# Six units' output rows evicted by ScalarE and added to x by GpSimd; V products one slot later, in a one-core encoder layer

## The chip, the cores and the metric

One Trainium2 chip, of which one core is used. The metric is the device time of one execution in microseconds, as the median of several runs; less is better. Beside the runs stands one profiled execution with its trace: each engine's instructions, their start, their length, and what ended the idle time before them. TensorE (PE in the profile, PEld its weight loads) multiplies, VectorE (DVE), ScalarE (ACT) and GpSimd (POOL) compute, SyncE (SP) issues nearly all transfers. Every engine works through its own instructions in order.

## The reference

One encoder layer over 1024 positions (a grid of 16 rows by 64 columns) of width 1024. x is RMS-normalised and projected to 3328 columns. Group A is attention of every position to every position (8 heads, 2 shared key/value heads, normalised and rotated q and k); group B lets a position see a window of 8 rows and 16 columns. Each group is multiplied by a SiLU gate, both are concatenated, projected once more, added to x and normalised:

```python
h = _rmsnorm(x, norm_gain[l])
proj = h @ w_in[l]
q_a, k_a, v_a, g_a, q_b, k_b, v_b, g_b = jnp.split(proj, split_at, axis=-1)
o_a = _gqa_blocked(q_a, k_a, v_a) * jax.nn.silu(g_a)
o_b = _neighbourhood_attn(q_b, k_b, v_b, na_rpb[l]) * jax.nn.silu(g_b)
x = x + jnp.concatenate([o_a, o_b], axis=-1) @ w_out[l]
return _rmsnorm(x, final_norm_gain)
```

(heads' reshapes, the norm and rotation of q_a and k_a left out). All is float32; the kernel splits every factor of a product into two float16 parts, high and low, and sums three products.

## The kernel before, in words

The 1024 positions are eight *units* of 128 rows (u); the unit's rows are chosen so that a unit of group B sees only itself and its neighbours, two units of keys at the borders, three elsewhere. Weights come in 17 groups of 256 columns: 0 to 12 of the first projection, 13 to 16 of the output projection. Every group is loaded (`load_w`), its sum of squares is formed in four quarters by ScalarE (`squares`, L372), and then it is split: high parts by ScalarE (L414), low parts by VectorE (L419). A unit's 24 matmuls with one group fill half a PSUM bank (`proj_tile`; two banks in turn in this stage, three in the tail).

The stage that the change touches is group B's (363 to 509 us): 32 *pairs* of heads, four for each unit in `ORDER` (0, 7, 1, 2, 3, 4, 5, 6). `run_units` walks through numbered *slots*. In slot i:

- `b_lo` (L863) forms the low half of pair i-1's weights on VectorE, and SP sends both halves through a transposing DMA (L865) into one of three `ptb` buffers;
- `b_qk` makes pair i's scores on TensorE (L833, L836), their biased row maxima on VectorE (L854), exponentials (L856) and high half (L858) on ScalarE;
- TensorE does about 4.2 *chunks* of fill, six matmuls each (L504): first the gate projections (groups 11 and 12), then the output projection, one *generator* of 8 chunks for two blocks of 128x256;
- `b_pv` multiplies pair i-3 with V on TensorE (L883 to L885). After four heads VectorE evicts the result (L892 to L895), GpSimd multiplies it with the gate (L897).

When a unit has both its halves, `os_start` squares, scales and splits its row of 1024 (L920, L925, L928, L933, L937) and SP transposes it (L946); these are the left factors of the output projection. An output generator (`out_gen`) ends with `then`, which files a job: `add` evicts the two blocks on VectorE, scaled row by row and added to x (L994). Then come squares of the finished half row on ScalarE (`fin_a`, L1019), the norm (`fin_b`, L1026 to L1030) and the store (L1031). x is loaded anew (`load_x2`, L984).

The order on an engine is that in which the program issues. `Flow.step` issues a slot: jobs of ScalarE up to 1.2 us of cost, then b_lo and b_qk, then the other jobs of ScalarE, jobs of VectorE, fill, and b_pv. A slot has a budget of 2.85 us for ScalarE's jobs and 2.45 for VectorE's (from `BASE_B`), of which up to half a budget is carried on; a job's `cost` is charged against it. Jobs with `late=0` always go in the slot where they are due, in the order of filing; others (squares of an output weight group: 1.0 each; its high parts 0.6, group 14's 0.3; its low parts 1.0) wait when the budget is short. The split of a unit's row counts 0.72 twice on ScalarE, `add` 0.5 a block on VectorE. Once a unit's job is filed it is due a slot later unless a delay is given.

Group B's stage ends with slot 34. Behind it the remaining output generators run back to back (the tail).

Of the kernel before, what the change touches and what calls it, by code (L numbers as in the profile page):

```python
# [8 lines left out]
F32 = mybir.dt.float32  # L9
F16 = mybir.dt.float16  # L10
BF16 = mybir.dt.bfloat16
AF = mybir.ActivationFunctionType
OP = mybir.AluOpType
# [3 lines left out]
P = 128  # L17
KC = 8
NU = 8
GC = 256  # L20
# [2 lines left out]
NX = 4  # L23
BASE_A, BASE_B = (1.72, 2.6, 2.8), (1.7, 1.6, 2.0)
HAND = 6
SKEW_A, SKEW_B = 5, 3
FILL_A = [(4, 5.0), (7, 4.2)]
FILL_A_END = 3.6
CHUNKS_A = 264
# [10 lines left out]
SLOTS = {"both": (16384, 2048, 4), "qc": (24576, 2048, 2), "stg1": (28672, 2048, 3), "stg": (18432, 2048, 3),  # L40
         "t": (0, 3072, 3), "ptb": (9216, 3072, 3), "th": (32896, 2048, 1), "y": (32896, 2048, 1),
         "p32": (AREA + 14464, 3072, 1)}
ORDER = (0, 7, 1, 2, 3, 4, 5, 6)
# [4 lines left out]
class Flow:  # L48
# [17 lines left out]
    def job(self, eng, cost, fn, *a, delay=1, late=1, key=None):  # L66

        self.jobs.append((late, self.slot + delay, self.number(), eng, cost, fn, a, key, self.tail))
# [83 lines left out]
def kernel(ctx: ExitStack, tc: tile.TileContext, x: bass.AP, w: bass.AP, wo: bass.AP,  # L152
# [3 lines left out]
    act, dve, pool, pe, sp = nc.scalar, nc.vector, nc.gpsimd, nc.tensor, nc.sync  # L156
# [3 lines left out]
    whl = ctx.enter_context(tc.tile_pool(name="whl", bufs=2))  # L160
# [7 lines left out]
    at, job = fl.at, fl.job  # L168
# [4 lines left out]
    def rows_of(t, u, width, off, n):  # L173

        return dap(t, 8 * u * width + off, [[64 * width, 16], [width, 8], [1, n]])
# [5 lines left out]
    def carve(store, off, shape, dt):  # L181

        n = 4 if dt == F32 else 2
        t = store[:, off // 4:off // 4 + int(np.prod(shape)) * n // 4]
        t = t if n == 4 else t.bitcast(dt)
        if len(shape) == 1:
            return t
        names = "abcdef"[:len(shape)]
        return t.rearrange(f"p ({' '.join(names)}) -> p {' '.join(names)}", **dict(zip(names, shape)))

    def area(off, shape, dt):
        return carve(ar, off + 16384, shape, dt)

    turn = {}

    def slot(kind, shape, dt):

        off, size, n = SLOTS[kind]
        k = turn[kind] = turn.get(kind, -1) + 1
        off += k % n * size  # L200
        return area(off, shape[1:], dt) if off < AREA else carve(rq, off - AREA, shape[1:], dt)
# [9 lines left out]
    def tn(name, n=1, tag="t"):  # L211
        return tiny.tile([P, n], F32, tag=tag, name=name)


    raw, wp, late, x2 = {}, {}, {}, {}
# [24 lines left out]
    for c in range(2):  # L240
        cs = slice(c * 512, (c + 1) * 512)
# [20 lines left out]
    def col(i, n=1):  # L262
        return sm[:, i:i + n]
# [65 lines left out]
    def proj_tile(name):  # L329
        if not banks:  # L330
            return ps_p.tile([P, 2, GC], F32, tag="pj", name=name)
        if not own:
            own.extend(ps_p.tile([P, 2, GC], F32, tag="pj", name=f"pjb{i}") for i in range(2))
        if "tail" in late and len(own) < 3:
            own.insert(0, banks[3].rearrange("p (a b) -> p a b", b=GC))
        own.append(own.pop(0))
        return own[-1]
# [117 lines left out]
    def need_w(g):  # L455
        if g not in scaled:
            fl.need(("sq", g), lambda: g in pend or g in scaled)
            fl.urgent()
            sums_now(True)
        fl.need(g, lambda: g in ready)  # L460
# [40 lines left out]
    def chunks(ops, n, then=None):  # L501
        for i in range(0, len(ops), n):
            for o in ops[i:i + n]:
                pe.matmul(*o[0], **o[1])  # L504
            if i + n >= len(ops):
                (then or sums_now)()
            elif 2 * i + 2 * n == len(ops) == 24 and n == 3:
                sums_now()
            yield
# [298 lines left out]
    def keys(u):  # L808

        a = max(u - 1, 0)  # L810
        return a, min(u + 1, NU - 1) - a + 1
# [49 lines left out]
    def b_lo(u, p):  # L861
        hl, p32 = hls.pop(("b", u, p))
        dve.scalar_tensor_tensor(hl[:, 1], p32, 2.0 ** 14, hl[:, 0], op0=OP.mult, op1=OP.subtract)  # L863
        pt = slot("ptb", [P, 4 * keys(u)[1], P], F16)
        sp.dma_start_transpose(pt, hl.rearrange("p a k -> p (a k)"))  # L865
        pts["b", u, p] = pt

    def b_pv(u, p):
        pt = pts.pop(("b", u, p))
        n = keys(u)[1]  # L870
        for e in range(2):
            b_pv_head(u, 2 * p + e, pt[:, e * n:e * n + n], pt[:, (2 + e) * n:(3 + e) * n])
# [108 lines left out]
    def load_x2(u):  # L981
        if u not in loaded:
            loaded.add(u)
            sp.dma_start(x2[u], rows_of(x, u, 1024, 0, 1024))  # L984

    def out_gen(jobs, done=()):

        pt = proj_tile(f"po{jobs[0][0]}_{jobs[0][1]}")
        rw = tn(f"rw{jobs[0][0]}_{jobs[0][1]}", 2, "rw")
        def add():  # L990
            for i, (u, g) in enumerate(jobs):
                cs = slice((g - 13) * GC, (g - 12) * GC)
                load_x2(u)
                dve.scalar_tensor_tensor(x2[u][:, cs], pt[:, i], rw[:, i:i + 1], x2[u][:, cs], op0=OP.mult, op1=OP.add)  # L994
        def then():
            job("dve", 0.5 * len(jobs), add, late=0)
            for u, h in done:
                job("act", 0.82, fin_a, u, h, delay=2, late=2)

        for i, (u, g) in enumerate(jobs):  # L1000
            need_w(g)
            fl.need(("os", u), lambda: u in mT)
            if i == 0 and jobs[-1] == (u, g + 1) and g + 1 in ready:
                dve.tensor_tensor(rw, col(RC + g, 2), rws[u][:, 3:4].to_broadcast([P, 2]), op=OP.mult)
            elif i == 0 or not both:
                dve.tensor_tensor(rw[:, i:i + 1], rws[u][:, 3:4], col(RC + g), op=OP.mult)
            both = i == 0 and jobs[-1] == (u, g + 1) and g + 1 in ready
            hi, lo = wp[g]
            seq = [(mT[u][a][:, k], b[:, k]) for k in range(KC) for a, b in ((0, hi), (0, lo), (1, hi))]
            yield from chunks([((pt[:, i], l, r), dict(start=n == 0, stop=n == 23))  # L1010
                               for n, (l, r) in enumerate(seq)], 6, then if i == len(jobs) - 1 else None)
# [52 lines left out]
    k, q = [kva_gen(up) for up in UP], group(1, [qa_gen(0, up) for up in UP])  # L1064
# [104 lines left out]
    ub = [(u, p) for u in ORDER for p in range(NH // 2)]  # L1169
# [27 lines left out]
    a, b = ORDER[2:4]  # L1197
# [7 lines left out]
    def hooks2(i):  # L1205
        hooks(i)
        for u, k in zip(ORDER, SPLIT_AT):
            if i - SKEW_B == k:
                at(0, "post", os_start, u)

    for u in ORDER[4:7]:
# [3 lines left out]
    def parts_b(i, back):  # L1215
        def first():
            if 1 <= i <= 32:
                b_lo(*ub[i - 1])
            if i < 32:
                b_qk(*ub[i])  # L1220
        return first, None, (lambda: b_pv(*ub[i - back])) if i >= back else None

    with run_units(32, SKEW_B, parts_b, rates(FILL_B, FILL_B_END), hooks2):
        pass
# [93 lines left out]
```

## Time and profile before

| | |
|---|---|
| median of 3 runs | 556.71 us (555.53 to 557.19) |
| the profiled execution | 558.52 us |
| its span, first to last instruction | 556.7 us |
| TensorE busy | 511.8 us, granted clock 0.981 on average |
| VectorE, ScalarE, GpSimd busy | 448.4, 373.5, 162.4 us |
| scores of pairs 0, 17 and 31 on TensorE | from 363.8, 430.2 and 494.0 us |
| last product with V | 508.5 us |
| last matmul | ends at 548.5 us |

In an instruction's row stand its start, its length, engine, line, operation, output<-inputs, shapes and the number merged into one row; in brackets the idle time of the engine before it and what ended it. Names are those of the storage: `ar`, `rq` and `rest` are arrays that hold many things by turns (transposed weights of attention, for one, are in `ar`), `pjb` and `sb` are PSUM banks, `whl` and `rest` hold split weights.

### The profile page before, as it was taken

To read this page: it belongs to the slowest core of one execution; us is meant where nothing else is said; L and a number is where in the kernel's file an instruction comes from. 1 tells how busy PE (TensorE), PEld (TensorE's weight loads), DVE (VectorE), ACT (ScalarE), POOL (GpSimd) and SP (SyncE) were. 2 spreads that over 40 slices of the span, in tenths; PEclk is the share of its full clock that TensorE was granted. 3 is DMA by queue.
4 is the path that set the end of the run, shared out by engine and by line. 5 is a ranking of instruction groups with operands and counts; after the bars stand their busy time and mean duration, and the time that the engine had idled before them with its cause. 6 is when DMAs were issued, how large, how long until landed. Compare 5 with 4: busy or idle time off the path is not lost.

```text
span 556.7 us, 12839 instructions
## 1 busy us (share of the span) xinstructions
PE 511.8 (92%) x5071; PEld 398.3 (72%) x5071; DVE 448.4 (81%) x911; ACT 373.5 (67%) x647; POOL 162.4 (29%) x185
## 2 busy tenths in 40 slices
PE   2667989989999999999999999999999989899994
PEld 0456878777887555568888888988777867688883
DVE  4599689789987988879879898777988988988532
ACT  5546465967887878787696796558688769662211
POOL 2385888571010000101001022633622211214000
PEclk9979999998999999999999999999999989999998
DMA  8998738779999999999997989644797999988612
GB/s 245 213 193 228 132 58 209 116 143 179 209 195 206 199 218 188 202 194 174 201 212 165 185 178 211 98 124 113 118 202 119 161 238 233 179 142 181 180 40 75
DMA packets 244509, 95.40 MB, mean 171 GB/s; under 512 B 235489, under 2 KB 236001, under 8 KB 242530
## 3 DMA queue, kind: packets, MB, share of 16 engines
q1 hardware_dynamic: 242434, 81.23, 78.3%
q0 software_dynamic: 1728, 12.58, 7.3%
q10 hardware_dynamic: 288, 0.79, 0.5%
q8 instruction: 39, 0.64, 0.5%
q14 instruction: 20, 0.16, 0.1%
HBM read 29.56 MB, written 4.19 MB: 61 GB/s over the span
## 4 chain that ended last, share of the span: by engine, by line
PE 52%; DVE 9%; ACT 6%; DMA 4%; issue 4%; POOL 1%; SPq 0%; DVEq 0%; POOLq 0%; ACTq 0%
PE pj L504 18%; PE pjb L504 8%; PE kb L504 7%; PE pv L775 5%; PE s L741 4%; PE s L743 4%; ACT rq L856 3%; PE pv L776 2%; DVE ar L854 2%; ACT ar L858 2%; PE sb L504 2%; DMA pt<-ar 2%; DMA x2b<-in_x_dram 1%; DVE ar L863 1%; DMA ar<-ar 1%
## 5 line engine op out<-in xcount | busy, mean ns | idle before, releaser
L504 PEld LDWEIGHTS <-hT 128*128 128x128 f16 x2112 | 204.3, 99 | 57.7 <-issue 16.0
L504 PE MATMUL pj<-whl,hT 128*128 128x256 f16 x1680 | 202.2, 279 | 20.2 <-DMA hT<-ar 7.5
L752 ACT ACTIVATE ar<-s,nm,sm 128x1024 f32<-128x1024 f32 x64 | 77.0, 1203 | 48.3 <-DVE nm L748 47.1
L748 DVE CUSTOM_DVE_ANT_0 ar<-s,sm 128x1024 bf16<-128x1024 f32 x64 | 81.9, 1280 | 30.1 <-PE s L743 28.4
L504 PEld LDWEIGHTS <-ar 128*128 128x128 f16 x768 | 74.5, 99 | 15.6 <-issue 4.5
L758 DVE TENSOR_TENSOR ar<-ar 128x1024 f16<-128x1024 f32 x64 | 79.1, 1237 | 1.4 <-ACT ar L753 1.3
L753 ACT ACTIVATE ar<-ar 128x1024 f16<-128x1024 f32 x64 | 67.6, 1057 | 2.3 <-DVE ar L758 0.4
L504 PE MATMUL pjb<-whl,ar 128*128 128x256 f16 x480 | 57.9, 277 | 3.1 <-DVE x2b L994 2.1
L856 ACT ACTIVATE rq<-ar,nm 128x384 f32<-128x384 f32 (+1 forms) x64 | 34.2, 580 | 32.8 <-DVE nm L854 32.1
L504 PE MATMUL pjb<-whl,hT 128*128 128x256 f16 x432 | 50.4, 273 | 0.1
L504 PE MATMUL kb<-hT,whl 128*128 128x512 f16 x192 | 44.5, 379 | 0.0
L784 POOL TENSOR_TENSOR ar<-ar,sum 128x256 f32<-128x256 f32 x16 | 11.4, 710 | 111.6 <-DVE ar L783 96.3
L419 DVE SCALAR_TENSOR_TENSOR whl<-raw,sm,whl 128x512 f16<-128x512 f32 x52 | 40.1, 798 | 2.8 <-ACT whl L414 2.8
L741 PE MATMUL s<-kTa,rq 128*128 128x512 f16 x128 | 38.5, 383 | 0.9 <-ACT ar L752 0.9
L775 PE MATMUL pv<-va,ar 128*128 128x128 f16 x384 | 39.3, 220 | 0.0
L775 PEld LDWEIGHTS <-ar 128*128 128x128 f16 x384 | 34.1, 98 | 5.5 <-issue 0.3
L776 PE MATMUL pv<-va,ar 128*128 128x64 f16 x384 | 38.0, 193 | 0.0
L897 POOL TENSOR_TENSOR ar<-ar,qkg 128x256 f32<-128x256 f32 x16 | 18.6, 1159 | 64.5 <-DVE qkg L895 63.2
L776 PEld LDWEIGHTS <-ar 128*128 128x128 f16 x384 | 33.4, 98 | 5.5 <-issue 0.3
L863 DVE SCALAR_TENSOR_TENSOR ar<-rq,ar 128x768 f16<-128x768 f32 (+1 forms) x32 | 30.5, 954 | 7.4 <-ACT ar L858 7.2
L414 ACT ACTIVATE whl<-raw,sm 128x512 f16<-128x512 f32 x52 | 34.0, 709 | 1.4 <-POOL sm L391 1.4
L391 POOL TENSOR_TENSOR sm<-wss,mh 128x1 f32<-128x1 f32 x17 | 10.5, 619 | 74.0 <-DVE wss L390 74.0
(165 smaller groups left out, 892.0 us busy)
## 6 DMA issues: line engine op xcount, KB each, us to landing
raw<-in_w_dram POOLq DMA_DIRECT2D x11, 1024.0 KB, 7.6
ar<-in_x_dram SPq DMA_DIRECT2D x7, 512.0 KB, 6.3
raw<-in_wo_dram SPq DMA_DIRECT2D x3, 1024.0 KB, 6.6
khh<-ar SPq DMA_DIRECT2D x16, 128.0 KB, 2.5
x2b<-in_x_dram SPq DMA_DIRECT2D x4, 512.0 KB, 6.9
x<-in_x_dram SPq DMA_DIRECT2D x4, 512.0 KB, 5.4
out_dram<-x2b SPq DMA_DIRECT2D x8, 256.0 KB, 3.7
out_dram<-x SPq DMA_DIRECT2D x7, 256.0 KB, 2.9
```

Source lines behind the costliest of these rows:

```text
L414: act.activation(wp[g][0][:, q], raw[g][:, q], AF.Copy, scale=col(S_ + g))
L419: dve.scalar_tensor_tensor(wp[g][1][:, q], raw[g][:, q], col(S_ + g), wp[g][0][:, q], op0=OP.mult, op1=OP.subtract)
L504: pe.matmul(*o[0], **o[1])
L741: pe.matmul(s[:, c * 512:(c + 1) * 512], q, kTa[:, 4 * c:4 * c + 4, hh], start=True, stop=False)
L748: dve.tensor_tensor_reduce(out=hl[:, 1].bitcast(BF16), in0=s, in1=col(SHA).to_broadcast([P, 1024]), scale=col(NSA), scalar=3e38, op0=OP.ad ...
L752: act.activation(p32, s, AF.Exp, bias=nm, scale=col(SCA), accum_out=rsum[hh, u][:, h:h + 1])
L753: at(0, "mid", lambda: act.activation(hl[:, 0], p32, AF.Copy))
L758: dve.tensor_tensor(hl[:, 1], p32, hl[:, 0], op=OP.subtract)
L775: pe.matmul(o, pt[:, kt], va[:, kt, hh], start=kt == 0, stop=False)
L776: pe.matmul(o[:, :D], pt[:, 8 + kt], va[:, kt, hh, :D], start=False, stop=kt == 7)
L856: act.activation(p32[:, e], t[:, e], AF.Exp, bias=nm, scale=-1.0)
L863: dve.scalar_tensor_tensor(hl[:, 1], p32, 2.0 ** 14, hl[:, 0], op0=OP.mult, op1=OP.subtract)
```

## The change

Three things. First, an output generator whose first unit is among the first six of `ORDER` and which ends after pair 17's `b_lo` files a job `put` for ScalarE in place of `add` for VectorE: two scaled copies out of PSUM into one of two float32 buffers, and GpSimd adds x to them, in one operation of 512 columns when both blocks belong to one unit, in two of 256 otherwise. These are twelve generators; the last two units in `ORDER` keep `add`. Second, pair i-3's product with V becomes pair i-4's from slot 18 on; slot 17 has none, and the stage gets one slot more. Third, the room for both: the buffer of split weights that held group 12 is taken again from pair 17 on, its first half as a fourth `ptb` buffer, its second as the two buffers of `put`. The moment at which `os_start` is first tried does not change; it is tried again a slot later when its unit isn't ready.

```diff
-SKEW_A, SKEW_B = 5, 3
+SKEW_A, SKEW_B, LATER = 5, 4, 17
...
     def b_lo(u, p):
         hl, p32 = hls.pop(("b", u, p))
         dve.scalar_tensor_tensor(hl[:, 1], p32, 2.0 ** 14, hl[:, 0], op0=OP.mult, op1=OP.subtract)
-        pt = slot("ptb", [P, 4 * keys(u)[1], P], F16)
+        shape = [P, 4 * keys(u)[1], P]
+        if ub.index((u, p)) >= LATER and "pt4" not in late:
+            late["pt4"] = whl.tile([P, 2, KC, GC], F16, tag="whl", name="pt4").rearrange("p a k c -> p (a k c)")
+            late["ov"] = late["pt4"][:, 2048:].bitcast(F32).rearrange("p (k a c) -> p k a c", k=2, a=2)
+            late["ring"] = [(LATER + k) % 3 for k in range(3)]
+            late["ring"].insert(0, 3)
+        if "ring" in late:
+            k = late["ring"][0]
+            late["ring"] = late["ring"][1:] + [k]
+            n = shape[1] * P
+            pt = (late["pt4"][:, :n].rearrange("p (a b) -> p a b", b=P) if k == 3 else
+                  area(SLOTS["ptb"][0] + k * SLOTS["ptb"][1], shape[1:], F16))
+        else:
+            pt = slot("ptb", shape, F16)
...
+        def put():
+            k = turn["ov"] = turn.get("ov", -1) + 1
+            o = late["ov"][:, k % 2]
+            for i in range(2):
+                act.activation(o[:, i], pt[:, i], AF.Copy, scale=rw[:, i:i + 1])
+            (u, g), (v, _) = jobs
+            for i, n in ((0, 2),) if u == v else ((0, 1), (1, 1)):
+                w = jobs[i][0]
+                cs = slice((g - 13) * GC, (g - 13 + n) * GC)
+                load_x2(w)
+                pool.tensor_tensor(x2[w][:, cs], x2[w][:, cs], o[:, i:i + n].rearrange("p a c -> p (a c)"), op=OP.add)
+
         def then():
-            job("dve", 0.5 * len(jobs), add, late=0)
+            if "ov" in late and jobs[0][0] in ORDER[:6]:
+                job("act", 0.4 * len(jobs), put, late=0)
+            else:
+                job("dve", 0.5 * len(jobs), add, late=0)
...
-            if i - SKEW_B == k:
+            if i - 3 == k:
                 at(0, "post", os_start, u)
...
-        return first, None, (lambda: b_pv(*ub[i - back])) if i >= back else None
+        j = i - back + (i < LATER)
+        return first, None, (lambda: b_pv(*ub[j])) if j >= 0 and i != LATER else None
```

## The prediction

> **What bounds the kernel now.** I read the engines' shares first, then the time in stretches, then who TensorE waits for, and last the instructions around those waits in order of time. On the page:
>
> ```profile
> PE 511.8 (92%) x5071; PEld 398.3 (72%) x5071; DVE 448.4 (81%) x911; ACT 373.5 (67%) x647; POOL 162.4 (29%) x185
> ```
>
> TensorE is the fullest engine. The change begins with pair 17, so only what lies behind about 434 us can move; stretches from there (columns: length, then busy us of PE, PEld, DVE, ACT, POOL, granted clock, DMA share, GB/s):
>
> ```profile
> 440.00:500.00 60.00, 54.59 (x621) 42.79 (x620) 53.16 (x145) 43.97 (x80) 9.98 (x12) 0.97 1.01 200
> 510.00:548.60 38.60, 38.49 (x353) 34.25 (x351) 19.60 (x53) 6.38 (x17) 4.96 (x8) 1.00 0.43 116
> 454.00:456.00 2.00, 2.00 (x12) 1.36 (x10) 1.53 (x5) 0.79 (x1) 0.30 (x1) 0.50 1.18 292
> ```
>
> From 510 us to its last product TensorE has no gap: the end is that product plus a fixed closing of 8.1 us. A microsecond of TensorE idleness removed between 440 and 510 us therefore shortens the kernel by one, as long as the tail stays full. In 440 to 500 us TensorE is idle for 5.4 of 60 us, VectorE for only 6.8. TensorE's waits from 434 to 512 us, and the places:
>
> ```profile
> PE pjb L504 <- DVE x2b L994: 2.4, 3, 1.7
> PE pvb L883 <- DMA ar<-ar: 2.3, 2, 1.8
> PE pjb L504 <- DVE whl L419: 0.9, 1, 0.9
> ```
> ```profile
> 451.99 0.20 PE L883 MATMUL pvb<-ar 128*128 128x65 f16 x1 [1.76 <-DMA ar<-ar]
> 453.24 3.79 PE L504 MATMUL pjb<-whl,ar 128*128 128x256 f16 x18
> 458.76 2.14 PE L504 MATMUL pjb<-rest,ar 128*128 128x256 f16 x18
> 466.62 0.20 PE L883 MATMUL pvb<-rq,ar 128*128 128x65 f16 x1 [0.54 <-DMA ar<-ar]
> 475.01 0.49 PE L833 MATMUL sb<-khh,qTb 128*128 128x384 f16 x2
> 478.88 0.49 PE L833 MATMUL sb<-khh,qTb 128*128 128x384 f16 x2
> 482.74 1.48 PE L504 MATMUL pjb<-whl,ar 128*128 128x256 f16 x12 [1.68 <-DVE x2b L994]
> 484.60 0.49 PE L833 MATMUL sb<-khh,qTb 128*128 128x384 f16 x2
> 487.08 2.67 PE L504 MATMUL pjb<-whl,ar 128*128 128x256 f16 x23 [0.85 <-DVE whl L419]
> 499.10 2.13 PE L504 MATMUL pjb<-whl,ar 128*128 128x256 f16 x18 [0.41 <-DVE x2b L994]
> 505.87 2.78 PE L504 MATMUL pjb<-rest,ar 128*128 128x256 f16 x24 [0.28 <-DVE x2b L994]
> ```
>
> Two waits are for a transposed pair (1.76 + 0.54 = 2.30 us), three for an output bank that VectorE has not emptied (1.68 + 0.41 + 0.28 = 2.37), one for weights (0.85). Behind the first, 18 matmuls take 3.79 us where 18 others take 2.14: the clock row above shows 0.50 there. That is 1.65 us more.
>
> **The change part by part.** *The product with V, one slot later.* Slot 17 issues none, slot 18 takes pair 14, and one slot is added at the end. No instruction is added; a slot's four fill chunks (24 matmuls, about 2.8 us) now lie in front of each product, more than both waits. I take 2.30 for them, and 1.65 for the slow stretch, since it follows the wait that goes (ends 0 and 1.65). The work of TensorE is the same: the extra slot draws its fill from the tail. The fourth buffer goes with the fourth slot, so each transpose finds its buffer free as early as now. Two places could pay for the move:
>
> ```profile
> 434.86 2.78 PE L504 MATMUL pjb<-whl,hT 128*128 128x256 f16 x24
> 438.37 0.95 DVE L863 SCALAR_TENSOR_TENSOR ar<-rq,ar 128x768 f16<-128x768 f32 x1
> 519.92 2.64 SPq L946 DMA_TRANSPOSE ar<-mhl  x2
> 537.85 2.78 PE L504 MATMUL pjb<-rest,ar 128*128 128x256 f16 x24
> ```
>
> The fourth buffer's space was the weights of group 12, last read by the first row, in slot 18's fill, until 437.6 us; VectorE gives pair 17's second half only at 439.3. I cost that wait at nothing; were it not covered, SP's queue would hold the next transposes. And from the fourth unit on each unit's output split starts a slot later. The last unit's transposes are issued by 522.6 us, TensorE first uses them at 537.9: a slot is covered several times.
>
> *The evictions.* Twelve pairs of 128x256 evictions leave VectorE, eight of them before 510 us. What they occupy there, and the first one's wait for x:
>
> ```profile
> 453.16 0.48 DVE L994 SCALAR_TENSOR_TENSOR x2b<-pjb,rw,x2b 128x256 f32<-128x256 f32 x1
> 454.40 0.48 DVE L994 SCALAR_TENSOR_TENSOR x2b<-pjb,rw,x2b 128x256 f32<-128x256 f32 x1 [0.76 <-DMA x2b<-in_x_dram]
> 463.02 0.87 DVE L994 SCALAR_TENSOR_TENSOR x2b<-pjb,rw,x2b 128x256 f32<-128x256 f32 x2
> 471.45 0.87 DVE L994 SCALAR_TENSOR_TENSOR x2b<-pjb,rw,x2b 128x256 f32<-128x256 f32 x2
> 481.27 0.61 DVE L854 CUSTOM_DVE_ANT_0 ar<-sb,rq,sm 128x384 f32<-128x384 f32 x1
> 486.29 0.74 DVE L419 SCALAR_TENSOR_TENSOR whl<-raw,sm,whl 128x512 f16<-128x512 f32 x1
> ```
>
> Merged, two take 0.87, one 0.48: they start 0.39 apart, a pair occupies 0.8, and the first with its wait 454.40 - 453.16 + 0.39 = 1.6. So three pairs before 481 us free 1.6 + 2 x 0.8 = 3.2 us. ScalarE's price comes from its copies out of PSUM, and from the same shape with a scale per row:
>
> ```profile
> L550 ACT ACTIVATE ar<-pj 128x256 f32<-128x256 f32 x4 | 1.5, 376 | 0.0
> L550 ACT ACTIVATE ar<-pj 128x512 f32<-128x512 f32 x8 | 4.7, 586 | 3.4 <-PE pj L504 3.4
> L706 ACT ACTIVATE ar<-pj,sm 128x512 f32<-128x512 f32 x7 | 4.7, 676 | 7.8 <-PE pj L504 7.8
> ```
>
> 0.376 + (0.676 - 0.586) = 0.47 us, 0.93 a pair. ScalarE idles 16 of the 60 us, before its exponentials, and the planner puts this job ahead of them unless 1.2 us of older jobs are there. So the bank is free after the exponentials of one pair, where VectorE frees it after the row maxima of the next: I take all 2.37 us of bank waits as gone. ScalarE is not idle everywhere:
>
> ```profile
> 464.00:468.00 4.00, 3.46 (x47) 2.50 (x45) 3.88 (x10) 3.92 (x11) 1.17 (x1) 1.00 1.23 213
> 468.00:472.00 4.00, 4.00 (x52) 3.23 (x51) 3.33 (x12) 3.97 (x8) 1.10 (x2) 1.00 1.10 243
> 482.60 0.84 ACT L858 ACTIVATE ar<-rq 128x768 f16<-128x768 f32 x1
> L414 ACT ACTIVATE whl<-raw,sm 128x512 f16<-128x512 f32 x52 | 34.0, 709 | 1.4 <-POOL sm L391 1.4
> ```
>
> From 464 to 472 us it is full, and a pair there lengthens the chain of exponentials by 0.9 (ends 0, if idle time takes it, and 6.5, if all seven before 506 us do).
>
> *The additions on GpSimd.* They are new there; nearest are its 256- and 512-wide operations of two arrays, and what one does to VectorE:
>
> ```profile
> L897 POOL TENSOR_TENSOR ar<-ar,qkg x16: 732/1166/1446, 392.3 to 513.9; 128x256 f32<-128x256 f32 x16
> L717 POOL TENSOR_TENSOR ar<-ar x8: 1270/1544/1713, 328.4 to 380.1; 128x512 f32<-128x512 f32 x8
> 435.45 1.88 DVE L937 SCALAR_TENSOR_TENSOR mhl<-ar,os,mhl 128x512 f16<-128x512 f32 x2
> 435.62 1.17 POOL L897 TENSOR_TENSOR ar<-ar,qkg 128x256 f32<-128x256 f32 x1 [3.03 <-DVE qkg L895]
> 519.11 1.41 DVE L937 SCALAR_TENSOR_TENSOR mhl<-ar,os,mhl 128x512 f16<-128x512 f32 x2
> ```
>
> GpSimd has 50 of 60 us free, so its own time costs nothing. But the two L937 take 1.88 us with L897 beside them and 1.41 without: 0.47 lost on VectorE. I take 0.5 a pair of evictions (ends 0 and the additions' whole shortest length, 2 x 0.73 = 1.46 or 1.27), as about half of VectorE's slot has such partners. Three pairs by 481 us give back 1.5 of the 3.2: VectorE is 1.7 us earlier there.
>
> [...] The eviction that is removed reads PSUM and one SBUF array. [...]
>
> *What caps it.* Up to slot 29 TensorE would gain 2.30 + 1.65 + 1.68 = 5.6 us. It can't begin a pair's scores before VectorE has read those two pairs back. Slot 29's scores start at 484.60, VectorE is through pair 27 at 481.27 + 0.61 = 481.88: 2.7 us of room, with VectorE's 1.7 less ScalarE's 0.9 that is 3.5. The weights of group 16 cap it lower. In slot 23 ScalarE's budget (2.85 us, up to 1.42 carried over) now bears an eviction and the moved split of a unit (0.8 + 1.44) beside the four squares of group 16 (4 x 1.0), so I expect two squares a slot later, and with them the weights' high parts behind slot 27's exponentials. Those end at 482.60 + 0.84 = 483.4; less 1.7, plus 0.9, plus two high parts (1.3) and the last low part (0.74) is 484.7. Now TensorE goes on at 487.08: a gain of 2.4 there (if nothing slips, the cap of 3.5; if the last low part stays a slot behind too, a loss, below). The later bank waits add 0.41 + 0.28 = 0.7.
>
> **The sum**: 2.4 + 0.7 = 3.1 us. The profiled execution took 558.52 us, 1.8 more than its span of 556.7; by chance the span equals the median of the runs, 556.71. So span 553.6, a profiled execution of 555.4, a median of 553.6.
>
> **The rivals.** *All idle time goes.* If locks and budgets cost nothing, 2.30 + 1.65 + 2.37 + 0.85 = 7.2 us: 549.5. For it: VectorE frees 3.2 us and the bank no longer hangs on it. Against: its room of 2.7 us, and every cap must open.
>
> *The lock eats it.* Each addition blocks VectorE for its shortest length: 1.46 + 1.46 + 1.27 = 4.2 by 481 us against 3.2 freed, so VectorE is 1.0 late; the weights end at 483.4 + 1.0 + 0.9 + 1.3 + 0.7 = 487.3, where TensorE stands now. What the later V products gain, TensorE waits again for weights and scores: 556.5, no change. For it: the 0.47 above. Against: the row maxima, which read PSUM, are much of VectorE's slot. [...]
>
> *Weights a slot late: slower.* Place: group 16's first use, slot 28. The squares slip, and VectorE's budget still leaves the last low part to the slot behind; a slot is 478.88 - 475.01 = 3.9 us. Then it ends not at 487.0 but at 490.9, and TensorE, in order, stands: 3.9 - 0.7 = 3.2 us slower, 559.9. It decides once that part ends more than 0.7 us behind 487.0. For it: it lies at 486.29, a slot behind its brothers, and 0.85 us are lost to it now. Against: VectorE's budget (2.45 a slot) loses the eviction's 1.0 that pushed it out.
>
> *It doesn't do what it says*: the V products wait anyway. The same late transpose would have to be late by a whole slot more, 3.9 us against 1.76 at worst; I fold it into no change.
>
> **How the numbers follow.** Forecast 0.50, between 551.2 and 555.0; everything goes 0.15; no change (the lock) 0.22; weights late 0.13. No change means within 0.3%, 1.7 us, which is about what a measurement of this kernel can tell. Faster 0.65, same 0.22, slower 0.13. The range reaches from 549.4, where all idle time goes, to 557.8, short of the late weights.
>
> **What would show it.** Right: no wait for transposes in front of L883 behind 440 us, no half clock near 454; bank waits of TensorE gone; ScalarE instructions of about 0.47 us at the new line; one wait left, for L419. Wrong: new waits for row maxima in front of L833, GpSimd additions over 2 us, longer L863 and L937 beside them, or L419 ending after 487 us.

## The result, and the profile after

The changed kernel takes 555.65 us (median of 20 runs, 553.08 to 558.62); the kernel before, on the same chip and over as many runs, 558.44 us. The ratio is 0.9949, 95% interval 0.9933 to 0.9966: 2.8 us faster, where 3.1 were forecast. (The forecast of 553.6 us started from a median of three runs, 556.71; over twenty runs the kernel before lies higher, so it is the difference that can be compared.) The profiled execution took 554.79 us, its span is 553.0. The engines' shares on its page:

```profile
PE 507.8 (92%) x5071; PEld 397.2 (72%) x5071; DVE 445.3 (81%) x887; ACT 381.4 (69%) x671; POOL 178.9 (32%) x201
```

VectorE lost 24 instructions, ScalarE gained 24, GpSimd 16. The stretches asked for before (length, then busy us of PE, PEld, DVE, ACT, POOL, granted clock, DMA share, GB/s):

```profile
440.00:500.00 60.00, 55.42 (x658) 44.75 (x657) 50.93 (x132) 48.67 (x95) 19.80 (x20) 1.00 1.05 197
508.00:545.00 37.00, 37.00 (x349) 32.98 (x344) 21.06 (x49) 10.08 (x27) 12.66 (x13) 1.00 0.49 128
```

In 440 to 500 us 37 more matmuls run than before, at full clock throughout; VectorE has gained 2.2 us of air, ScalarE has lost 4.7. The tail is full, as it was. TensorE's waits from 434 to 512 us, in total and then where they lie:

```profile
PE pjb L504 <- ACT pt L1013: 1.8, 1, 1.8
PE pjb L504 <- ACT whl L414: 1.5, 2, 0.7
PE pjb L504 <- DVE whl L419: 1.3, 2, 0.8
PE pjb L504 <- DVE ar L712: 0.3, 1, 0.3
```
```profile
469.62 1.47 PE L504 MATMUL pjb<-rest,ar 128*128 128x256 f16 x12 [1.80 <-ACT pt L1013]
478.25 0.27 PE L504 MATMUL pjb<-whl,ar 128*128 128x256 f16 x1 [0.74 <-ACT whl L414]
479.32 0.71 PE L504 MATMUL pjb<-whl,ar 128*128 128x256 f16 x5 [0.80 <-DVE whl L419]
480.75 0.27 PE L504 MATMUL pjb<-whl,ar 128*128 128x256 f16 x1 [0.72 <-ACT whl L414]
481.54 0.71 PE L504 MATMUL pjb<-whl,ar 128*128 128x256 f16 x5 [0.52 <-DVE whl L419]
```

The two waits for transposes are gone, and so are VectorE's bank waits. One bank wait is left, on ScalarE's new instruction (L1013), and TensorE now meets the weights of group 16 quarter by quarter, as they are made. The last quarters' low parts on VectorE, and the matmuls of that group behind the next pair's scores:

```profile
480.73 2.08 DVE L419 SCALAR_TENSOR_TENSOR whl<-raw,sm,whl 128x512 f16<-128x512 f32 x3 [1.47 <-ACT whl L414]
483.32 3.45 PE L504 MATMUL pjb<-whl,ar 128*128 128x256 f16 x30
```

**A yardstick for single executions.** Where the last stage begins differs between executions of the same program: pair 0's scores start between 361.9 and 368.3 us in the profiles of this study. From there to pair 17's scores it is 66.4 to 66.6 us in every one, and from the last matmul to the end of the span about 8. So I measure from pair 17's scores, where the change begins, to the end of the last matmul. In the changed kernel these are the rows

```profile
429.54 0.49 PE L833 MATMUL sb<-khh,qTb 128*128 128x384 f16 x2
542.26 2.78 PE L504 MATMUL pjb<-whl,ar 128*128 128x256 f16 x24
```

that is 545.04 - 429.54 = 115.50 us; before, it was 548.49 - 430.19 = 118.30. The difference of 2.80 us is as large as that of the medians, but by chance: 1.7 of it is time at half clock, which this execution of the changed kernel has none of and another one (e8, below) has 3.0 of.

### The profile page after: what moved, and what is told of

Read it like the earlier page. It is cut to its first block, busy times and chain, and to the rows that moved or that the text cites. A ratio compares the mean times of both kernels' runs of the same rounds, so it can differ in the third digit from the quotient of the medians.

```text
span 553.0 us, 12864 instructions
## 1 busy us (share of the span) xinstructions
PE 507.8 (92%) x5071; PEld 397.2 (72%) x5071; DVE 445.3 (81%) x887; ACT 381.4 (69%) x671; POOL 178.9 (32%) x201
## 4 chain that ended last, share of the span: by engine, by line
PE 50%; DVE 10%; ACT 9%; issue 5%; DMA 3%; POOL 0%; DVEq 0%; POOLq 0%; ACTq 0%
PE pj L504 17%; PE kb L504 7%; PE pjb L504 7%; PE pv L775 5%; PE s L741 4%; PE s L743 4%; ACT rq L856 3%; DVE ar L854 3%; ACT ar L858 2%; PE pv L776 2%; PE sb L504 2%; DMA pt<-ar 2%; DVE ar L863 1%; DMA ar<-ar 1%; DVE whl L419 1%
## 5 line engine op out<-in xcount | busy, mean ns | idle before, releaser
L504 PE MATMUL pjb<-whl,ar 128*128 128x256 f16 x480 | 56.4, 273 | 2.8 <-ACT whl L414 1.5
L419 DVE SCALAR_TENSOR_TENSOR whl<-raw,sm,whl 128x512 f16<-128x512 f32 x52 | 41.0, 821 | 2.7 <-ACT whl L414 2.7
L775 PE MATMUL pv<-va,ar 128*128 128x128 f16 x384 | 39.1, 220 | 0.0
L863 DVE SCALAR_TENSOR_TENSOR ar<-rq,ar 128x768 f16<-128x768 f32 (+1 forms) x32 | 29.3, 915 | 11.0 <-ACT ar L858 10.6
L910 POOL TENSOR_TENSOR ar<-ar,qkg 128x256 f32<-128x256 f32 x16 | 17.1, 1072 | 51.6 <-DVE qkg L908 36.4
```

The lines of the kernel that those rows point to most:

```text
L419: dve.scalar_tensor_tensor(wp[g][1][:, q], raw[g][:, q], col(S_ + g), wp[g][0][:, q], op0=OP.mult, op1=OP.subtract)
L775: pe.matmul(o, pt[:, kt], va[:, kt, hh], start=kt == 0, stop=False)
```

## The experiments

All runs stand in this table. *Stretch* is the yardstick in the run's one profiled execution; *waits* is the sum of TensorE's waits from 434 to 512 us (without L712's 0.2 to 0.3, which all have); *half clock* is what TensorE lost to a granted clock of about 0.5, as the sum of busy time times (1 - granted clock) over stretches of 1 us.

| run | ratio (95%) | stretch | waits | half clock |
|---|---|---|---|---|
| before | 1 | 118.30 | 5.6 | 1.7 |
| changed | 0.9949 (0.9933–0.9966) | 115.50 | 4.6 | 0 |
| e1 skew only | 0.9973 (0.9947–0.9998) | 116.82 | 4.4 | 1.7 |
| e2 evict only | 0.9987 (0.9968–1.0006) | 118.84 | 6.3 | 1.7 |
| e3 put uncharged | 0.9911 (0.9879–0.9944) | 114.76 | 3.8 | 0 |
| e4 no x added | 0.9950 (0.9922–0.9979) | 115.64 | 3.5 | 1.5 |
| e5 uncharged, ahead | 0.9896 (0.9870–0.9922) | 114.42 | 2.2 | 1.7 |
| e6 additions twice | 0.9990 (0.9968–1.0011) | 117.87 | 5.3 | 1.6 |
| e7 squares late | 0.9904 (0.9870–0.9938) | 114.20 | 2.0 | 1.6 |
| e8 changed, again | 0.9959 (0.9935–0.9982) | 117.75 | 4.2 | 3.0 |
| e9 sums behind | 0.9968 (0.9949–0.9988) | 117.51 | 4.4 | 2.9 |
| e10 ahead, charged | 0.9992 (0.9968–1.0016) | 117.17 | 4.5 | 1.6 |
| e11 sums a slot later | 0.9930 (0.9908–0.9952) | 114.35 | 3.4 | 0 |
| e12 evict only, free | 0.9975 (0.9958–0.9992) | 117.51 | 5.3 | 1.6 |

The last two columns account for the third: waits and half clock together are 7.3 us before and 4.6 after, 2.7 less where the stretch shows 2.80; e3 gives 3.5 less against 3.54, e11 3.9 against 3.95. No run is off by more than 0.8 us. The column on half clock is an upper estimate: all runs have the same 1214 matmuls in the stretch, TensorE is busy for 110.5 to 110.6 us of it at full clock and for 112.8 in e9, 2.2 to 2.3 more where the column has 2.9. So what is to be explained is which waits there are, and when half clock follows one.

**e1: the skew alone.** Products with V one slot later, all evictions on VectorE.

```diff
-            if "ov" in late and jobs[0][0] in ORDER[:6]:
+            if False:
```

> The V product a slot later and the fourth buffer, every eviction on VectorE as before. My theory: the waits for transposes in front of the V products (1.76 and 0.54 us before) and the half clock near 454 us go, but TensorE then stands for the output banks that VectorE still empties at its old pace (1.68 us before at 482.7 us grows by what was gained in front of it), so the kernel gains 0 to 1 us: ratio 0.998 to 1.000. Rival A, the whole gain is the later V product: ratio 0.995, and the bank waits stay at 2.4 us in sum. Rival B, the later product does nothing because TensorE waits for the same transposes one slot on: 1.000 with waits in front of the V product left.

TensorE's waits in e1:

```profile
PE pjb L504 <- DVE x2b L1007: 3.2, 2, 2.0
PE pjb L504 <- DVE whl L419: 1.2, 1, 1.2
```

No wait for a transpose is left: the fourth slot covers them by itself. The bank waits on VectorE grew from 2.4 to 3.2, as TensorE comes to VectorE's evictions sooner. And behind the first of them (1.98 us, at 454.00) the clock is halved (same columns as above):

```profile
454.00:459.00 5.00, 5.00 (x43) 3.52 (x43) 4.90 (x14) 2.79 (x5) 2.43 (x2) 0.66 1.19 243
```

(1 - 0.66) x 5.00 = 1.7 us, the loss that the kernel before has behind its transpose wait. The skew took away the wait, and the half clock found another one.

**e2: the eviction alone.** Products three slots behind throughout, no fourth buffer.

```diff
-SKEW_A, SKEW_B, LATER = 5, 4, 17
+SKEW_A, SKEW_B, LATER = 5, 3, 17
...
-        if "ring" in late:
+        if False:
...
-        j = i - back + (i < LATER)
+        j = i - back
```

> Evictions by ScalarE and additions on GpSimd, the V product three slots behind as before and three buffers. My theory: the bank waits (2.37 us before) go or shrink, the waits for transposes (2.30 us) stay, the weights of group 16 come a slot late as in the changed kernel (2.8 us of waiting there), so 0.5 to 1.5 us are gained: ratio 0.997 to 0.999. Rival A (the whole gain is the later product, the moved evictions are neutral or cost): ratio 1.000 or above. Rival C (the evictions alone make the gain): 0.995.

```profile
PE pvb L896 <- DMA ar<-ar: 4.3, 2, 2.7
PE pjb L504 <- DVE whl L419: 1.8, 2, 1.4
PE pjb L504 <- ACT pt L1013: 0.2, 1, 0.2
```

The bank waits are gone (0.2 left), and the time with them went into the waits for transposes: 4.3 us where the kernel before has 2.3, with half clock behind the longer one. No gain is measured. Each half of the change by itself lets TensorE run into the wait that the other half removes. But what the evictions add to the skew is not shown: e1 waits 4.4 us, the changed kernel 4.6; without half clock e1's stretch is 115.1 us, the changed kernel's 115.5; and the ratios (0.9973 against 0.9949 and, in e8, 0.9959) have intervals that overlap.

**e3: the put without its charge.** `put` costs nothing in ScalarE's budget, so the squares of weight group 16 (L372) need not slip a slot.

```diff
-                job("act", 0.4 * len(jobs), put, late=0)
+                job("act", 0.0, put, late=0)
```

> The changed kernel with the eviction job charged 0 to ScalarE's budget in place of 0.8, so the four squares of group 16 stay in slot 23 and its high parts come a slot earlier. My theory: the four waits of TensorE for group 16's parts (0.74 + 0.80 + 0.72 + 0.52 = 2.8 us in the changed kernel) shrink below 1 us and 1.5 to 2.5 us more are gained: ratio 0.990 to 0.992. Rival: TensorE then stands as long elsewhere (scores, banks), since VectorE's and ScalarE's pace decides: 0.995, like the changed kernel, with new waits named in front of the scores or the output groups.

ScalarE's rows for the squares and high parts of group 16, first in the changed kernel, then in e3:

```profile
462.90 0.61 ACT L372 ACTIVATE rest<-raw 128x512 bf16<-128x512 f32 x1
463.64 0.63 ACT L372 ACTIVATE rest<-raw 128x512 bf16<-128x512 f32 x1
464.40 0.63 ACT L372 ACTIVATE rest<-raw 128x512 bf16<-128x512 f32 x1
...
477.49 0.71 ACT L414 ACTIVATE whl<-raw,sm 128x512 f16<-128x512 f32 x1
...
479.99 1.93 ACT L414 ACTIVATE whl<-raw,sm 128x512 f16<-128x512 f32 x3
```
```profile
463.54 0.63 ACT L372 ACTIVATE rest<-raw 128x512 bf16<-128x512 f32 x1
464.29 0.63 ACT L372 ACTIVATE rest<-raw 128x512 bf16<-128x512 f32 x1
...
466.80 0.61 ACT L372 ACTIVATE rest<-raw 128x512 bf16<-128x512 f32 x1
467.54 0.63 ACT L372 ACTIVATE rest<-raw 128x512 bf16<-128x512 f32 x1
...
479.19 2.54 ACT L414 ACTIVATE whl<-raw,sm 128x512 f16<-128x512 f32 x4
```

Counted from pair 17's scores (429.54 and 432.87), the high parts begin 48.0 and 50.5 us later in the changed kernel and 46.3 in e3, all four together. The 2.8 us of waiting for the group's parts are gone. New waits take most of their place, so that the stretch is 0.74 us shorter than the changed kernel's (114.76 against 115.50, both without half clock). The ratio is about 0.4% lower (0.9911 against 0.9949 and 0.9959), 2 us and more, but over seven runs and with intervals that overlap. TensorE's waits in e3 are all for ScalarE, which is nearly full in the stretch where they lie:

```profile
PE pjb L504 <- ACT pt L1013: 2.1, 2, 1.7
PE sb L388 <- ACT rest L372: 1.7, 2, 1.1
```
```profile
464.00:484.00 20.00, 16.58 (x194) 13.05 (x193) 15.61 (x43) 18.67 (x40) 7.04 (x9) 1.00 1.14 205
```

**e4: no x added.** GpSimd's additions are left out, so in the rows of six units the output is the normalised x without its product; the evictions still run.

```diff
-                pool.tensor_tensor(x2[w][:, cs], x2[w][:, cs], o[:, i:i + n]..., op=OP.add)
```

> The changed kernel without the sixteen additions on GpSimd: x is left without the product in the first six units, so their rows come out wrong; ScalarE's evictions, their buffers and all else stay. It prices the additions. My theory (0.5 us of VectorE's time lost for each eviction pair, 7 pairs before the last V product, partly covered): 0.5 to 1.5 us faster than the changed kernel, ratio 0.992 to 0.994; VectorE's operations with two arrays in SBUF show no instance lengthened by a 512-wide addition (L938 of 1.86 us in the changed kernel back at 0.75). Rival (the additions lie beside VectorE for nothing): 0.995 as the changed kernel. Rival (each addition blocks for its whole length, 1.27 to 1.46 us, on the path): 0.987.

The ratio is that of the changed kernel. In its profile the stretch is 115.64 us, 1.5 of them half clock behind a wait for L419; without that it would be 114.1 to 114.5 (TensorE's busy time grew by 1.2), 1.0 to 1.4 us below the changed kernel. The medians average over such events and show no difference, 0.3% either way. What an addition did to VectorE in one place can be read off. VectorE's L938 (two arrays in SBUF), then GpSimd's addition beside it, in the changed kernel; last, all L938 of e4 (shortest, median and longest in ns):

```profile
469.60 1.86 DVE L938 CUSTOM_DVE_ANT_0 rest<-ar,os 128x512 bf16<-128x512 f32 x1
```
```profile
469.64 1.27 POOL L1019 TENSOR_TENSOR x2b<-x2b,pt 128x512 f32<-128x512 f32 x1 [2.95 <-ACT pt L1013]
```
```profile
L938 DVE CUSTOM_DVE_ANT_0 rest<-ar,os x5: 743/749/752, 430.3 to 502.0; 128x512 bf16<-128x512 f32 x5
```

1.86 - 0.75 = 1.1 us lost to an addition of 1.27. This isn't rare: VectorE has 219 instructions in the stretch in both runs and is busy for 87.80 us with the additions, for 80.10 without. That is 7.7 us, 0.5 for each of the 16, though much of it lies where TensorE waits for nothing (L1059, from 501 us on, takes 13.3 us for 10.1 in e4).

**e6: the additions twice.** A second addition of the same size behind each, on the evicted rows, which are spent by then.

```diff
+                spent = o[:, i:i + n].rearrange("p a c -> p (a c)")
+                pool.tensor_tensor(spent, spent, spent, op=OP.add)
```

> The changed kernel with every GpSimd addition of x followed by a second one of the same size on the evicted rows, which are spent by then: about 20 additions, some 24 us, more on GpSimd, the output is the same. Theory A (the additions cost by holding up VectorE's instructions between two SBUF buffers, seen as 1.86 us in place of 0.75 at 469.6 us): the stretch from pair 17's scores to the last matmul grows from 115.50 by 1 to 1.5 us, what the run without additions is worth if its half clock at 480 us (1.7 us) is taken out; ratio 0.997 to 0.9985; L938 and L419 show more instances above 1.2 us. Rival B (VectorE has slack enough there, or GpSimd's time is free): no change, 115.2 to 115.8, ratio 0.994 to 0.996. Rival C (GpSimd becomes the bound of os's chain through the pow of L941 behind the additions): TensorE waits for transposes (pjb <- DMA mT) appear, 3 us and more, ratio above 1.0.

There are 16 more GpSimd instructions, 15.6 us of its busy time. The stretch without its half clock is 117.87 - 1.6 = 116.3, 0.8 us above the changed kernel's; the medians are 558.00 against 556.43 on the same chip, 1.6 us more, with intervals that overlap. No wait for transposes appeared. VectorE is busy for another 4.8 us (92.61). So the medians put the additions at somewhere between nothing and 1.6 us; as each ratio is uncertain by some 0.2 to 0.3%, a cost of up to about 3 us is not excluded.

**e8: the changed kernel again.**

> The changed kernel itself, beside the others on one chip. Theory A (the part of the time that the stages set is the same in every execution, and only the start of the last stage and the clock behind some of TensorE's waits differ): 17 to end 115.5 within 0.3 us unless TensorE is granted half clock behind one of its waits, which adds 1.7 us; ratio 0.995 within 0.002. Rival B (the last stage varies by itself by 1 us and more between executions): another stretch time without a half clock to account for it.

The ratio agrees (0.9959), the profile of this execution doesn't: 117.75 us in place of 115.50. Its waits are the same ones, to the hundredth in three of four:

```profile
477.49 0.27 PE L504 MATMUL pjb<-whl,ar 128*128 128x256 f16 x1 [0.74 <-ACT whl L414]
478.55 0.71 PE L504 MATMUL pjb<-whl,ar 128*128 128x256 f16 x5 [0.80 <-DVE whl L419]
479.98 0.37 PE L504 MATMUL pjb<-whl,ar 128*128 128x256 f16 x1 [0.72 <-ACT whl L414]
480.77 1.23 PE L504 MATMUL pjb<-whl,ar 128*128 128x256 f16 x5 [0.42 <-DVE whl L419]
...
483.99 4.57 PE L504 MATMUL pjb<-whl,ar 128*128 128x256 f16 x30
```
```profile
479.00:487.00 8.00, 6.86 (x49) 4.42 (x47) 6.20 (x15) 5.46 (x11) 0.72 (x1) 0.57 0.98 169
```

Five matmuls take 1.23 us where they took 0.71. The same program with much the same waits gets half clock in one execution and none in the other: TensorE is busy 2.69 us longer (113.33 against 110.64) and idle 0.44 less, mostly for a bank wait of 1.46 in place of 1.80. Together that is the 2.25 us.

**e5 and e10: the put ahead of ScalarE's other work in its slot**, without its charge and with it.

```diff
-            due = sorted((j for j in due if j[0] == 0 or j[4] / 2 < self.left[eng] - kept),
+            due = sorted((j for j in due if j[0] <= 0 or j[4] / 2 < self.left[eng] - kept),
...
-                job("act", 0.4 * len(jobs), put, late=0)
+                job("act", 0.0, put, late=-1)
```

(in e10 the charge stays at `0.4 * len(jobs)`).

> The eviction on ScalarE (put) carries no charge, as in the run that only took the charge away, and also goes ahead of the other work due on ScalarE in its slot (of two squares' sums and of four squares of finished rows). Theory A: TensorE's remaining waits for ScalarE come from the place of the put in ScalarE's order. Then the time from pair 17's scores to the last matmul falls below the 114.76 us of the run without the charge, by the part of its 2.1 us of waits for the put that the new place removes, to some 113 to 114.5 us, and the ratio to the kernel before is 0.988 to 0.991. Rival B: the put at 482 us there stands behind four weight products (L414) of the slot before, which its place within a slot does not change, and the gain of the run without the charge came from the slots' budgets alone. Then the stretch stays within 0.5 us of 114.76 and the ratio within 0.003 of that run's.

> The changed kernel, its put with its charge of 0.8 but ahead of what else is due on ScalarE in its slot. Theory A (the charge is what delays the squares of weight group 16 by a slot and so the group's high parts; the place of the put only sets the bank waits): the wait for the put (1.5 to 1.8 us at 469 us) goes, the waits for the group's parts (about 2.8 us in all, at 478 to 482 us) stay; 17 to end 113.5 to 114 us without a half clock, 1.5 to 3 us more with one; ratio 0.992 to 0.9945. Rival B (place alone did it): all waits as in the run with the put uncharged and ahead, ratio 0.988 to 0.991.

e5 is the fastest kernel of the study: 552.19 us over six runs, 0.9896 of the kernel before, and faster than the changed one by interval too. The waits for the put, 2.1 us in e3, are gone; what is left are L388's, 1.41 and 0.59, with half clock behind them. e10, in contrast, gained nothing (0.9992): the put's place alone removes none of the waits. Without its half clock the stretch is 115.5 us, the changed kernel's; why its median lies higher than that kernel's is open.

```profile
PE pjb L504 <- DVE whl L419: 2.1, 2, 1.6
PE pjb L504 <- ACT pt L1013: 1.5, 1, 1.5
PE pjb L504 <- ACT whl L414: 0.9, 2, 0.7
```

I had expected of the place that it takes the wait for the put away, with or without the charge. It does not in e10, since that put still stands behind the exponentials of its slot, 39.1 us behind pair 17's scores as in the changed kernel (39.2). Between e10 and e5, which differ in the charge alone, lies 1% (0.9992, 0.9896): the charge is what counts.

**e7: squares of finished rows late.** As e5, and L1048 is due in slot 34 and not two slots behind its row.

```diff
-                job("act", 0.82, fin_a, u, h, delay=2, late=2)
+                job("act", 0.82, fin_a, u, h, delay=max(2, late.get("end", 0) - fl.slot), late=2)
...
+            late["end"] = fl.slot + 34
```

> As the run with the put uncharged and ahead, and the squares of the finished rows (L1048, 0.82 us each on ScalarE, eight of them) are due in slot 34 instead of two slots after their rows are complete. Theory A (ScalarE's order sets the remaining waits): TensorE's waits for ScalarE between 434 and 512 us fall by 0.5 to 1.5 us against the run with the put uncharged and ahead, and the ratio by 0.001 to 0.003. Rival B (ScalarE has air in these slots, the squares hide): no difference beyond 0.001. Rival C: the squares now crowd the slots 34 and 35 ahead of the last units' evictions, and TensorE, which never waits between 510 and 545 us in the changed kernel, waits there for a bank 1 to 3 us: ratio higher by 0.002 to 0.005.

No difference to e5 (0.9904 against 0.9896; the stretches are 114.20 and 114.42). These squares lay in ScalarE's air.

**e9 and e11: the sums of group 16's squares moved on TensorE**, both on top of e5's edits, as they try to take e5's last waits. In e9 the four matmuls (L388) go to the end of their slot:

```diff
-            prep_b(g, at_s[:, 400 + g:401 + g])
-            try_split(g)
+            sums = lambda: (prep_b(g, at_s[:, 400 + g:401 + g]), try_split(g))
+            at(0, "end", sums) if g == 16 else sums()
```

> As the run with the put uncharged and ahead, and the four small matmuls that add up the squares' sums of weight group 16 (L388) stand at the end of their slot, behind its products, instead of right behind its scores; the split of the group is still due a slot later. Theory A: of the 2.0 us that TensorE waits there (1.41 and 0.59 us) nearly all goes, since the last of ScalarE's four sums ends at 463.8 us and the slot's products take TensorE some 3.5 us longer; with the wait goes the half clock behind it (1.7 us). The time from pair 17's scores to the last matmul falls from 114.42 to 110.7 to 112.5 us and the ratio from 0.9896 to 0.983 to 0.987. Rival B: the wait is only moved to the next engine in the chain, the split of the group comes later by the slot's 3.5 us and TensorE waits for the group's high and low parts (whl) near 478 us: 113.5 to 114.5 and a ratio of 0.988 to 0.991.

```profile
469.70 0.27 PE L388 MATMUL sb<-wss,mh 128*128 128x1 bf16 x4 [4.40 <-DVE nm L854]
```

Neither theory: the sums share a bank with the scores, and at the end of the slot they wait for VectorE's row maxima (L854), which read that bank: 4.40 us, and half clock of 2.9. In e11 they go behind the next pair's scores, whose bank isn't read yet:

```diff
-                job("act", 0, pend.append, g, delay=2 if "b" in late else 1, ...)
+                job("act", 0, pend.append, g, delay=(3 if g == 16 else 2) if "b" in late else 1, ...)
...
-            job("act", 0.3 if g == 14 else 0.6, hi, i, late=0.5 ...)
+            job("act", 0.3 if g == 14 else 0.6, hi, i, delay=int(g != 16), late=0.5 ...)
```

> As the run with the put uncharged and ahead; the matmuls that add up the squares' sums of weight group 16 (L388) and the two small steps behind them (L390, L391) stand one slot later, right behind the next pair's scores, where their bank has not been read yet; the order on ScalarE through the high parts (L414) is the same, whose scale is then ready some 4 us later but still ahead of them. Theory A (TensorE's wait of 2.0 us there, and the half clock behind it, are what that run has left to lose): wait and half clock are gone, the time from pair 17's scores to the last matmul is 110.7 to 112.5 us, the ratio 0.983 to 0.987. Rival B: another wait takes its place (the high parts at 474 us wait for the scale, or the scores for their bank): 113 to 114.5 us and 0.987 to 0.991.

L388 doesn't wait any more, and the clock is full. But TensorE, which comes earlier, waits for the put again:

```profile
PE pjb L504 <- ACT pt L1013: 3.4, 2, 2.5
```
```profile
477.52 2.54 ACT L414 ACTIVATE whl<-raw,sm 128x512 f16<-128x512 f32 x4
479.98 0.61 ACT L1048 ACTIVATE ar<-x2b 128x512 bf16<-128x512 f32 x1
480.50 0.18 ACT L1048 ACTIVATION_READ_ACCUMULATOR ar<-x2b 128x1 f32 x1
480.59 0.81 ACT L1013 ACTIVATE pt<-pjb,rw 128x256 f32<-128x256 f32 x2
```

The put at 480.59 stands behind four high parts, issued late in the slot before, and one square. The stretch is e5's (114.35 against 114.42), the ratio no better (0.9930). In e5 this put starts as late, 49.1 us behind pair 17's scores for 49.0 here. So e5's order did not remove the waits for the put: L388's wait and the half clock, 3.7 us, hid them. What TensorE waits for there is ScalarE's work; the order only says at which instruction.

**e12: the eviction alone, uncharged and ahead**: e2's and e5's edits together.

> The eviction on ScalarE with its addition on GpSimd alone, products three slots behind throughout and one ring of spaces as in the kernel before, with the put uncharged and ahead. Theory A (the eviction by itself gained nothing because products three slots behind come ahead of their transposed probabilities, which TensorE waited 4.3 us for in the run with the eviction alone, and the charge has no part in that): the wait for transposed probabilities (pv <- DMA) of 3 us and more stays, with a half clock behind it or not; 116.5 to 119 us from pair 17's scores to the last matmul, ratio 0.995 to 1.0. Rival B (the charge ate the eviction's gain, and the fourth slot is worth little once it is gone): 114 to 115.5 us, ratio 0.989 to 0.994.

```profile
PE pvb L896 <- DMA ar<-ar: 4.9, 2, 3.1
PE pvb L896 <- DVE x2b L1059: 0.4, 1, 0.4
```

The waits for transposes stay, 4.9 us; 0.9975 against e2's 0.9987. So it was not mainly the charge that kept the eviction from gaining: the waits for transposes stand as they did. A small gain remains (0.25%, interval below 1), in which e12 and e2 can't be told apart.

## Why the prediction was right

The forecast, its sign and its size held, and so did most of its steps; some of them held by compensation, and that the profiled executions differ by as much as the medians is luck. (Prediction and trace have different starting points: pair 17's scores are at 430.19 us in the kernel before, at 429.54 in the changed one.)

- *The product with V, one slot later.* Right as to the waits: 2.30 us of them gone, in e1 as in the changed kernel, and nothing paid at the fourth buffer (its first transpose was issued at 438.77 us and took 1.42, as the one before the change). **The 1.65 for the slow stretch was the wrong kind of term.** I booked it as removed with its wait. It is a chance event behind any of several waits: e1 has 1.7 us of it behind a bank wait, e8 3.0 at the waits for weights, the first profile of the same kernel none. The sum did not need the 1.65, as the weights capped the gain below it.
- *The eviction.* 0.458 us in the median, where 0.47 was worked out; a pair 0.82, for 0.93.
- *All 2.37 us of bank waits gone.* Too much: VectorE's are gone, but 1.80 us on ScalarE took the place of one. The prediction saw the stretch (464 to 472 us, ScalarE full) and priced the pair there as 0.9 us on the chain of exponentials, at either side of it. It did not ask when the put itself would be reached. Three squares, two halves of finished rows, a pair's exponentials and a half of a unit's row (L933) are ahead of it, and TensorE stood for its bank.
- *The additions.* They do hold VectorE up, in one place by more than the 0.5 us a pair that I took from L937: L938 took 1.86 us where e4 has 0.75, 1.1 lost beside an addition of 1.27 that starts 0.04 us behind it. Not every instruction is held: of the row maxima (L854), which read PSUM, one at 487.81 us lies beside an addition (487.77 us, 1.27) for its whole length and takes 0.61 us, and none of the changed kernel's 64 takes more than 0.62. What decides it, no run shows. The 0.5 us a pair was near the mark for VectorE's own time (7.7 us for the twelve pairs, 0.64 each), but little of it reached TensorE. The rival in which each addition costs its whole shortest length, 4.2 us by 481, fell: leaving out the additions brought no difference in the medians, doubling them 1.6 us.
- *The weights cap.* Right in its mechanism: three squares of group 16 (two in the prediction) came after the next exponentials, three of the four high parts behind those of slot 27, as worked out from the budgets, and e3 shows that the charge did it. The size came out right too, but not by the wait that was foreseen. The matmul that first reads the last low part, the eighth behind slot 29's scores, began 56.89 us behind pair 17's scores before and begins 54.55 behind them now (484.09 us, in the row of 30): 2.34 us gained, for 2.4. It doesn't wait, since that part ends 1.3 us ahead of it (482.81). TensorE takes the quarters as they come, and it was held by the earlier ones: only one wait for the group was foreseen, L419's; there are four, 2.8 us in all. And 0.55 of the 2.34 is a product with V that is still owed there and is paid later (slot 17, which has none, takes 3.32 us, its neighbour before the change 3.87); the sum has no term for it.
- *The scores cap* was never reached; TensorE waits for no row maxima.

The sum of 2.4 + 0.7 stands against 2.80: 2.34 at the weights, less the product that is owed, plus the two later bank waits (0.69) and 0.3 us that I can't place. In e8, with the same waits and half clock on top, the same matmul begins 56.37 us behind pair 17's scores, a gain of 0.5; so the good agreement of the single steps is one draw. Of the rivals, the one in which all idle time goes was stopped by the put and the weights, as said; the late weights went the way that it describes, by a slot, but with the high parts and not with the last low part, and so cost only the difference to e3.

What stays open: why half clock falls behind one wait and not behind its twin. And where most of the medians' 2.8 us comes from. Waits account for 1.0 of it (5.6 against 4.6 us; 1.4 in e8). Less half clock on average is not the answer, as far as the record tells: each run's granted clock over the whole execution is known, and its mean is 0.981 over the changed kernel's twenty runs (0.975 to 0.989, the profiled one being the highest) and 0.983 over the 100 runs of the kernel before that stand beside the experiments. What the additions cost is known only as said at e6.

## What to carry to other kernels

Where two waits follow each other closely on the engine that sets the end, removing one can lengthen the other, as in e1 and e2; a ledger of that engine's waits, and of the clock behind them, before and after tells where the time went. Work moved to an engine with air by the average still has an order there: ask what stands ahead of it in the slot where its result is wanted, and what its charge in a planner pushes out of that slot, since here the charge moved the time more than the place did (e10 and e5). A single profile with a half clock in it, or without, is one draw, even where it agrees with the medians; compare stretches that begin where the change begins, with that loss set apart.

## What the runs showed of the hardware that was not expected

Half clock followed short waits of TensorE: behind 1.76 us in the kernel before, 1.98 in e1, 1.41 and 0.59 in e5, and from the third of the four short waits of e8 on (0.74, 0.80, 0.72, 0.42). It did not follow the 1.80 us of the changed kernel, nor the 2.46 of e11. When it came, it mostly lasted about 3.4 us (1.7 lost at a granted clock of 0.50; in the kernel before from 453.5 to 456.9 us), in e8 and e9 about twice that (3.0 and 2.9 lost). The length of the wait ahead does not tell whether it comes (1.76 and 1.98 us with it, 1.80 and 2.46 without), and of two executions of the changed kernel with nearly the same waits, 4.6 and 4.2 us in all, one had it and one had not. What starts it, no run shows.

And the last stage begins at times 6 us apart in executions of programs that are alike up to there, 361.9 in e5 and 368.3 in e7, while the 66.5 us behind it repeat within 0.2. Spans of single executions say nothing about a change of this size.
